# Seven raw weight buffers in place of four, in space taken from the scratch of the software DMAs

## The chip, the cores and the metric

The kernel runs on one core of one Trainium2 chip. The engines of a core work side by side: TensorE (PE in the profile, with its weight loader PEld), VectorE (DVE), ScalarE (ACT), GpSimd (POOL) and SyncE (SP), which here only starts transfers. Sixteen DMA engines move data between HBM and the on-chip memory SBUF. The metric is the device time of one execution in microseconds; lower is better.

## The reference

Two decoder layers over 256 tokens of width 2048, all in float32. The first layer has block attention over 16 heads, the second grouped-query attention (4 shared key/value heads, window 128, a learned sink per head). With 256 tokens and blocks of 256, the first layer's attention is plain causal attention. Each layer ends in a gated feed-forward with a causal depthwise convolution of width 3 between the up projection (2048 to 2 x 5504) and the gate:

```python
h = x
for layer in range(2):
    attn = moba_attention(...) if layer == 0 else swa_attention(...)      # q, k, v, softmax(q k + bias) v, w_o
    h = layer_norm(sqrt(2) * h + attn, ln_g[layer, 0], ln_b[layer, 0])
    ffn = conv_ffn(h, w_up, conv_w, conv_b, w_down)                       # (gelu(conv(h w_up)_g) * conv(h w_up)_v) w_down
    h = layer_norm(sqrt(2) * h + ffn, ln_g[layer, 1], ln_b[layer, 1])
```

Every weight is used once, for 256 tokens: the work is a stream of weights from HBM against a small resident activation.

## The kernel before, in words

**The stream.** The host lays out all weights in the order of use as "halves" of 128 x 1024 float32 (512 KB). There are 704 halves from the input `wst`; 68 more, named `t`, are sums of four blocks of the down projections' weights, which the kernel itself forms in HBM (below). One half after the other goes through three steps:

1. `load_weights` (lines 101 to 109): SP starts the DMA of half `u` into a buffer of the pool `wpool`, which has `RAW_BUFS` = 4 buffers. The tile is `raw`, the DMA is line 106.
2. `high_upto` (line 125): ACT rounds `raw` to the faster matmul format, giving `wh`. `low_piece` (line 134): DVE subtracts, giving the remainder `wl`. These have `HALF_BUFS` = 4 buffers of their own; near the ends of a stage further halves are put into tiles that are free just then (`xT`, `up`, `st`).
3. TensorE multiplies with `wh` and `wl`, three products for each one of float32. In the stages with `ws_unit` (lines 294 and 297), two halves are one unit: 16 matmuls with 512 columns and 16 with 256. The down projections use lines 555 to 557 (`two_chunks`), and their last part, like the value and output projections, lines 347 to 349 (`Moving.mm`).

**Order.** The order of each engine's instructions is written out by the program (`manual_schedule`). `take()` hands out half `i`; before that `split_upto` writes the high and low parts up to half `i + 3`, and after the split of half `s` it writes the next `load_weights`. That next load is half `s + 4` and reuses the buffer of `s`, so it waits on SP until DVE has read it. `at(n, f)` puts other work `n` halves later in this order. SP works through its queue in order, and so a wait there holds what is behind it. Each SP transfer is also given one of eight semaphores in turn, and waits until the transfer that had it before has landed.

**Also on SP:** the pieces of the input `xc` (line 187), tables for the bias, the bias bands of the first layer (lines 278 and 282), the residual input (213), the layer-norm vectors (437).

**The sums.** `plan_sums` spreads over each up projection the making of the sums `t` for the down projection after it (16 for the first layer, 18 for the second, each of two halves). A sum starts with two plain copies on SP (line 261). Then POOL starts three accumulating DMAs in turn (lines 263, 265 and 267), each of which waits for the one before. [...] POOL also starts the second layer's band and bias transfers, four of each in a row, the convolution's weights and some layer-norm vectors; apart from that it does next to nothing.

**Stages in order:** first attention, with its input loaded and split at the start (`load_input`) to 300 us; its output projection to 390; up projection of the first layer to 860; its down projection to 1080; second attention to 1260 and output projection to 1350; second up projection to 1840; second down projection and the final layer norm to the end.

Of the kernel before, what the change touches and what calls it, by code (L numbers as in the profile page):

```python
# [33 lines left out]
SCALE = P ** -0.5  # L34
UL = 384

RAW_BUFS = 4
HALF_BUFS = 4
AHEAD = HALF_BUFS - 1
HW = 1024  # L40
# [34 lines left out]
def trunk(ctx: ExitStack, tc: tile.TileContext, wst, wq, xT_in, x_in, relb, onehot, umask, sinks, conv_in, ln_g, ln_b, out):  # L75
    nc = tc.nc
# [3 lines left out]
    big = ctx.enter_context(tc.tile_pool(name="big", bufs=1))  # L80
    wpool = ctx.enter_context(tc.tile_pool(name="wpool", bufs=RAW_BUFS))
    spool = ctx.enter_context(tc.tile_pool(name="spool", bufs=HALF_BUFS))
# [18 lines left out]
    def load_weights(behind=None):  # L101
        u = todo["load"]
        if u < n_halves:
            raws[u] = wpool.tile([P, HW], F32, name="raw")
            for j, c in enumerate(pieces(u)):
                nc.sync.dma_start(raws[u][:, c], source[u][:, c])
                if behind:
                    behind(j)
            todo["load"] += 1
# [26 lines left out]
    def split_upto(i, behind=None):  # L136
        while todo["low"] <= min(i, n_halves - 1):
            s = todo["low"]
            high_upto(s, behind)
            if len(pieces(s)) == 1:  # L140
                low_piece(s, slice(0, HW))
            placed.pop(s)
            raws.pop(s)
            load_weights()
            todo["low"] += 1
# [4 lines left out]
    def at(n, f, *a, first=False):  # L150

        fs = before.setdefault(slot["now"] + n, [])
        fs.insert(0 if first else len(fs), (f, a))
# [29 lines left out]
    def load_input(pool, tables):  # L183
        xc = pool.tile([P, KB, T], F32, name="xc", bufs=1)

        def load_x(k, n=2, queue=nc.sync):
            queue.dma_start(xc[:, k:k + n], xT_in[:, k:k + n, :])

        def split_x(k, n=2):
            ks = slice(k, k + n)  # L190
            nc.scalar.activation(xT[:, ks, 0:T], xc[:, ks], AF.Copy)  # L191
            nc.vector.tensor_tensor(out=xT[:, ks, T:2 * T], in0=xc[:, ks], in1=xT[:, ks, 0:T].bitcast(F32),
                                    op=ALU.subtract)

        load_weights(lambda j: load_x(j, 1, nc.scalar))
        for u in range(1, RAW_BUFS):
            load_weights()
            if u < 3:
                load_x(u + 1, 1)
        load_x(4)  # L200
        load_x(6)
        tables()
        split_upto(0, lambda j: split_x(j, 1))
        for u in range(1, 3):
            split_upto(u)
            split_x(u + 1, 1)
        for k in range(4, KB, 2):
            if k > 6:
                at(k - 7, load_x, k)
            at(k - 3, split_x, k)  # L210

    def load_residual(t):
        nc.sync.dma_start(res[:, t, :], x_in[t * P:(t + 1) * P, :])
# [518 lines left out]
    def layer_attention(l, rest, stage, turnover):  # L732
# [29 lines left out]
        if l == 0:  # L762
            load_input(pool, lambda: bias_table(pool))
        else:
            nc.vector.tensor_scalar(nsk, sk, -1.0, None, op0=ALU.mult)
# [293 lines left out]
```

## Time and profile before

| | |
|---|---|
| median of 3 runs (lowest, highest) | 2072.65 us (2072.06, 2077.46) |
| the profiled execution, whole | 2069.8 us |
| its span | 2067.6 us |
| busy: TensorE / weight loader / VectorE / ScalarE / GpSimd | 2052.7 / 1771.9 / 1548.5 / 1038.0 / 112.1 us |
| mean granted TensorE clock | 0.998 |
| moved by DMA | 512.07 MB, mean 248 GB/s |
| landing of a raw half from its issue, median | 5.3 us |

In the rows that follow, L12 is line 12 of the kernel, `wh<-raw` is what is written and read, "x" a count, and `A <- B: total, times, longest` says that A sat idle until B. A matmul's end is modelled: consecutive matmuls overlap, so the spacing of their starts tells the pace and the duration does not. SPq is SP's queue. In a row of a stretch, the busy time and count of each engine follow, then the granted clock, the DMA engines' busy share and GB/s. "q1" are transfers of SP, "q0" those of POOL.

### The profile page before, as it was taken

How to read it: one execution, taken by the hardware profiler on the slowest of the kernel's cores; microseconds unless marked ns; L12 is line 12 of the kernel's file. 1: busy time of each engine (PE TensorE's matmuls, PEld its weight loads, DVE VectorE, ACT ScalarE, POOL GpSimd, SP SyncE). 2: the span in 40 equal slices, each digit the busy share in tenths (PEclk: the TensorE clock that was granted, in tenths of full speed). 3: DMA queues.
4: the chain of work that ended last, by engine and by line, in shares of the span. 5: the costliest groups of instructions: out<-in, count | busy, mean ns of one | idle time of the engine just before them, and what ended most of it. 6: DMA issues, size and time to landing. Idle time of an engine off the chain costs nothing.

```text
span 2067.6 us, 29230 instructions
## 1 busy us (share of the span) xinstructions
PE 2052.7 (99%) x10974; PEld 1771.9 (86%) x10974; DVE 1548.5 (75%) x2292; ACT 1038.0 (50%) x1467; POOL 112.1 (5%) x124
## 2 busy tenths in 40 slices
PE   9999999999999999999999999999999999999997
PEld 7888888988888888887888888898888888888886
DVE  5555556788787888877776676788887788886867
ACT  5544444444454455565564555444444445556553
POOL 0000000001111110000000000001111111100000
PEclk9999999999999999999999999999999999999999
DMA  8666548389999998588885544739999999969884
GB/s 320 211 209 210 173 164 280 133 244 288 294 302 274 307 267 263 184 278 294 281 290 195 182 149 160 251 109 302 289 303 309 301 303 262 261 219 308 289 292 160
DMA packets 158445, 512.07 MB, mean 248 GB/s; under 512 B 17840, under 2 KB 22512, under 8 KB 157536
## 3 DMA queue, kind: packets, MB, share of 16 engines
q1 hardware_dynamic: 131168, 456.56, 63.4%
q0 software_dynamic: 26848, 53.39, 15.2%
q8 instruction: 86, 1.41, 0.3%
q14 instruction: 55, 0.45, 0.1%
q10 hardware_dynamic: 288, 0.26, 0.0%
HBM read 507.97 MB, written 86.56 MB: 288 GB/s over the span
## 4 chain that ended last, share of the span: by engine, by line
PE 85%; DMA 8%; DVE 4%; ACT 2%; issue 1%; ACTq 0%; DVEq 0%
PE acc L294 35%; PE acc L297 18%; DMA raw<-in_wst_dram 7%; PE acc L348 5%; PE acc L347 5%; PE acc L349 5%; PE acc L556 3%; PE acc L557 3%; PE acc L555 3%; DVE wl L134 3%; ACT wh L125 2%; PE acc L312 1%; DMA raw<-t 1%; PE at L556 1%; PE at L557 1%; PE at L555 1%
## 5 line engine op out<-in xcount | busy, mean ns | idle before, releaser
L134 DVE TENSOR_TENSOR wl<-raw,wh 128x1024 fp32r<-128x1024 f32 (+1 forms) x716 | 871.2, 1219 | 436.6 <-ACT wh L125 428.0
L125 ACT ACTIVATE wh<-raw 128x1024 fp32r<-128x1024 f32 (+1 forms) x716 | 754.7, 1055 | 681.3 <-DMA raw<-in_wst_dram 309.2
L294 PE MATMUL acc<-xT,wh 128*128 128x512 f32 x3456 | 872.9, 394 | 0.1
L294 PEld LDWEIGHTS acc<-xT,wh 128*128 128x128 f32 x3456 | 623.5, 189 | 113.4 <-ACT wh L125 0.4
L297 PEld LDWEIGHTS acc<-xT,wl 128*128 128x128 f32 x3456 | 471.2, 190 | 34.1 <-DVE wl L134 0.4
L297 PE MATMUL acc<-xT,wl 128*128 128x256 f32 x3456 | 481.8, 282 | 0.0
L556 PE MATMUL acc<-wl,up 128*128 128x512 f32 x336 | 130.9, 390 | 0.8 <-DVE wl L134 0.8
L555 PE MATMUL acc<-wh,up 128*128 128x512 f32 x336 | 130.9, 390 | 0.0
L557 PE MATMUL acc<-wh,up 128*128 128x512 f32 x336 | 130.8, 389 | 0.0
L885 DVE SCALAR_TENSOR_TENSOR work<-work,cw 128x255 f32<-128x255 f32 x172 | 83.2, 484 | 6.1
L886 DVE SCALAR_TENSOR_TENSOR work<-work,cw 128x254 f32<-128x254 f32 x172 | 83.1, 483 | 6.2
L162 ACT ACTIVATE work<-work 128x256 f32<-128x256 f32 x86 | 35.7, 415 | 94.0 <-DVE work L886 93.8
L884 DVE TENSOR_SCALAR work<-work,cw 128x256 f32<-128x256 f32 x172 | 71.6, 417 | 6.2
L556 PEld LDWEIGHTS acc<-wl,up 128*128 128x128 f32 x336 | 63.1, 188 | 14.1 <-DVE wl L134 1.1
L555 PEld LDWEIGHTS acc<-wh,up 128*128 128x128 f32 x336 | 63.1, 188 | 13.6 <-ACT wh L125 0.5
L557 PEld LDWEIGHTS acc<-wh,up 128*128 128x128 f32 x336 | 63.1, 188 | 13.1
L883 DVE TENSOR_TENSOR work<-acc,work 128x256 f32<-128x256 f32 x172 | 71.7, 417 | 1.5 <-ACT work L882 1.5
L882 ACT ACTIVATE work<-acc 128x256 f32<-128x256 f32 x172 | 62.6, 364 | 6.5 <-PE acc L324 6.5
L347 PE MATMUL acc<-wh,xT 128*128 128x512 f32 x144 | 57.6, 400 | 0.6 <-ACT xT L191 0.6
L263 POOL DMA_DIRECT2D t<-in_wq_dram x34 | 44.4, 1305 | 240.4 <-DMA t<-in_wq_dram 240.3
L265 POOL DMA_DIRECT2D t<-t x34 | 35.1, 1032 | 397.6 <-DMA t<-in_wq_dram 361.9
L348 PE MATMUL acc<-wl,xT 128*128 128x512 f32 x144 | 56.3, 391 | 0.0
(208 smaller groups left out, 2148.0 us busy)
## 6 DMA issues: line engine op xcount, KB each, us to landing
raw<-in_wst_dram SPq DMA_DIRECT2D x704, 512.0 KB, 5.3
t<-in_wq_dram SPq DMA_DIRECT2D x68, 512.0 KB, 8.9
raw<-t SPq DMA_DIRECT2D x68, 512.0 KB, 4.7
t<-in_wq_dram POOLq DMA_DIRECT2D x34, 512.0 KB, 12.7
t<-t POOLq DMA_DIRECT2D x34, 512.0 KB, 9.4
t<-in_wq_dram POOLq DMA_DIRECT2D x34, 256.0 KB, 7.7
gb<-in_ln_g_dram POOLq DMA_DIRECT2D x2, 1024.0 KB, 10.5
gb<-in_ln_b_dram POOLq DMA_DIRECT2D x2, 1024.0 KB, 13.4
```

The source lines that it names most:

```text
L125: nc.scalar.activation(wh[:, c], raws[s][:, c], AF.Copy)
L134: nc.vector.tensor_tensor(out=wl[:, c], in0=raws[s][:, c], in1=wh[:, c].bitcast(F32), op=ALU.subtract)
L294: nc.tensor.matmul(acc, cols(wh, j), xT[:, k, :], start=(k == 0), stop=False)
L297: nc.tensor.matmul(o, cols(wl, j), xT[:, k, 0:T], start=False, stop=(k == KB - 1))
L347: nc.tensor.matmul(acc, sh, wh, start=(k == 0), stop=False)
L348: nc.tensor.matmul(acc, sh, wl, start=False, stop=False)
L349: nc.tensor.matmul(acc, sl, wh, start=False, stop=(k == self.nk - 1))
L555: nc.tensor.matmul(bank(key), a[0], wh[:, c], start=key not in begun, stop=False)
L556: nc.tensor.matmul(bank(key), a[0], wl[:, c], start=False, stop=False)
L557: nc.tensor.matmul(bank(key), a[1], wh[:, c], start=False, stop=stop)
L885: nc.vector.scalar_tensor_tensor(c[:, 1:T], h[:, 0:T - 1], w[:, 1:2], c[:, 1:T], op0=ALU.mult, op1=ALU.add)
L886: nc.vector.scalar_tensor_tensor(c[:, 2:T], h[:, 0:T - 2], w[:, 0:1], c[:, 2:T], op0=ALU.mult, op1=ALU.add)
```

## The change

The raw pool gets seven buffers of 4 KB a partition in place of four. The 12 KB for that come from the DMA scratch, which is set to 4 KB. At the start four halves are loaded ahead as before; three further `load_weights` calls are put in the order after halves 16, 19 and 22. From there on the load written after the split of half `s` is half `s + 7`. Since buffers rotate by seven from the first half on, the fifth to seventh loads find free buffers and have no split to wait for. Every tile allocated before the raw pool lies 12 KB lower; those after it stay.

```diff
-RAW_BUFS = 4
+RAW_FIRST = 4
+RAW_BUFS = 7
+DMA_SCRATCH = 4096
...
         load_weights(lambda j: load_x(j, 1, nc.scalar))
-        for u in range(1, RAW_BUFS):
+        for u in range(1, RAW_FIRST):
             load_weights()
...
             at(k - 3, split_x, k)
+        for i in range(RAW_BUFS - RAW_FIRST):
+            at(16 + 3 * i, load_weights)
...
-    nc = _bacc.Bacc("TRN2", target_bir_lowering=False, num_devices=1)
+    nc = _bacc.Bacc("TRN2", target_bir_lowering=False, num_devices=1, dynamic_dma_scratch_size=DMA_SCRATCH)
```

## The prediction

> **What bounds the kernel now.** I read the page first, then who waited for whom (all engines, then the weight loader and SP's queue), the matmul counts by stretch, and the order of time around the few places where TensorE waits. The page:
>
> ```profile
> span 2067.6 us, 29230 instructions
> PE 2052.7 (99%) x10974; PEld 1771.9 (86%) x10974; DVE 1548.5 (75%) x2292; ACT 1038.0 (50%) x1467; POOL 112.1 (5%) x124
> ...
> DMA  8666548389999998588885544739999999969884
> ...
> raw<-in_wst_dram SPq DMA_DIRECT2D x704, 512.0 KB, 5.3
> ```
>
> TensorE (PE) looks busy for 99% of the span, but its ends are modelled, so I check that with matmul counts. The two long stretches in which the DMA engines are fullest are the up projections; line 294 is 16 of a unit's 32 matmuls:
>
> ```profile
> 416.00:860.00 444.00, 318.71 (x1272) 228.69 (x1272) 1.00 0.93 273
> 1390.00:1830.00 440.00, 315.70 (x1262) 226.55 (x1260) 1.00 0.98 287
> ```
>
> 444 us over 1272/16 units is 5.585 us a unit; 440 over 1262/16 is 5.578. The second stretch has a higher DMA share (0.98 against 0.93) and is no slower. The matmuls set this pace, and a fuller queue has not moved it. The granted clock is 1.00 in both.
>
> Now what the weight buffers cost. Columns: us in total, times, longest.
>
> ```profile
> ACT wh L125 <- DMA raw<-in_wst_dram: 309.2, 245, 5.0
> ...
> ACT wh L125 <- DMA raw<-t: 37.2, 44, 2.7
> ...
> PE acc L556 <- DVE wl L134: 0.8, 1, 0.8
> ...
> PE acc L348 <- DVE wl L134: 0.4, 1, 0.4
> ```
>
> ScalarE (ACT) waits 309.2 + 37.2 = 346 us for raw weights; TensorE waits 1.2 us. Between them stand the four `wh`/`wl` pairs, three halves ahead, which is some 8 us of matmul. So the raw ring is late all the time for ACT and hardly ever for the engine that sets the end. The weight loader shows the same waits before the matmul queue smooths them:
>
> ```profile
> PEld acc L556 <- DVE wl L134: 1.7, 3, 1.1
> ...
> PEld acc L348 <- DVE wl L134: 1.1, 2, 0.8
> PEld at L556 <- DVE wl L134: 0.9, 3, 0.4
> ...
> PEld acc L555 <- ACT wh L125: 0.5, 1, 0.5
> PEld acc L294 <- ACT wh L125: 0.4, 2, 0.3
> PEld acc L297 <- DVE wl L134: 0.4, 2, 0.2
> ```
>
> The two large ones, in order of time (start, duration):
>
> ```profile
> 949.68 0.39 PE L557 MATMUL acc<-wh,up 128*128 128x512 f32 x1
> ...
> 950.11 0.49 PE L555 MATMUL acc<-wh,up 128*128 128x512 f32 x1
> ...
> 951.37 0.50 PE L556 MATMUL acc<-wl,up 128*128 128x512 f32 x1 [0.76 <-DVE wl L134]
> ...
> 951.71 0.40 PE L557 MATMUL acc<-wh,up 128*128 128x512 f32 x1
> ...
> 951.95 0.40 PE L555 MATMUL acc<-wh,up 128*128 128x512 f32 x1
> ```
> ```profile
> 2042.81 0.39 PE L347 MATMUL acc<-wh,up 128*128 128x512 f32 x1
> ...
> 2043.61 0.50 PE L348 MATMUL acc<-wl,up 128*128 128x512 f32 x1 [0.41 <-DVE wl L134]
> ...
> 2043.94 0.40 PE L349 MATMUL acc<-wh,up 128*128 128x512 f32 x1
> ```
>
> Matmuls of this shape otherwise start 0.23 us apart (951.71 to 951.95 is 0.24). From 949.68 to 951.71, three steps that should take 0.69 took 2.03: 1.34 lost. From 2042.81 to 2043.94, two steps took 1.13 in place of 0.46: 0.67 lost. Together 2.0 us.
>
> **The change, part by part.**
>
> *The ring of seven.* Nothing is computed more or less. All engines but SP keep the order of their instructions; SP issues the same loads, earlier. Why ACT waits now is in the chain of waits, one turn of the ring:
>
> ```profile
> 897.74 5.54 DMA raw<-in_wst_dram
> ...
> 903.39 1.07 ACT wh L125
> ...
> 904.48 1.24 DVE wl L134
> ...
> 905.73 5.02 DMA raw<-in_wst_dram
> ```
>
> Load, high half, low half, then the freed buffer's next load: 905.73 − 897.74 = 7.99 us for four halves, 2.00 us a half. With seven buffers the same turn gives 1.14 us a half, and one transfer alone has the next bound: 512 KB at the 296 GB/s of the fullest stretch is 1.77 us. So in the down projections a half can come about 0.2 us sooner, until the ring is full, and each stage is entered with three more halves in hand (three times about 2.3 us). ACT's wait for raw should mostly go; late next are its waits for a free `wh` buffer, that is for TensorE. What TensorE gets back: the 2.0 us above, and part of the small waits. The loader rows that wait on `wh` or `wl`, without the 0.3 us of line 348 that lies in the opening, sum to 1.7 + 0.8 + 0.9 + 0.5 + 0.4 + 0.4 = 4.7; of that, 2.4 (0.5 + 1.1 + 0.8) belongs to the two places counted. The other 2.3 lies in small waits, which a loader one matmul ahead partly absorbs; I take half, 1.2. Gain: 2.0 + 1.2 = **3.2 us**, between 2.0 and 4.7.
>
> *Three more loads, after halves 16, 19 and 22.* Three DMA issues of about 0.33 us on SP, which does nothing else. 3 × 512 KB is 4.9 us of DMA at the opening's rate, and in the order written the loads 4 to 6 no longer wait for a split, so they go out at once behind the first four:
>
> ```profile
> 0.00:50.00 50.00, 48.02 (x210) 39.15 (x211) 27.83 (x34) 26.81 (x35) 2.95 (x10) 1.00 0.89 321
> 9.11 8.12 SPq L106 DMA_DIRECT2D raw<-in_wst_dram  x5
> ```
>
> They ride SP's queue, behind everything needed sooner, and SP reaches the input pieces queued after them no later than now. Cost 0; if their transfers did push the input back, up to 4.9 us.
>
> *Order past SP's queue.* SP also carries the first two transfers of each sum (line 261), the bias table, the residual and the layer-norm vectors. They keep their place in the order but land behind up to three more halves, some 5 us (3 × 1.77). The sums have long cover, below; the others are loaded stages ahead.
>
> *SP's own limits.*
>
> ```profile
> SPq L106 <- DVE wl L134: 695.7, 373, 8.9
> ...
> SPq L106 <- DMA raw<-in_wst_dram: 81.2, 65, 3.5
> ```
>
> SP waits mostly for a split to free a buffer. But 65 times it waited for an earlier load to land: the written order gives each SP transfer one of eight semaphores, which the transfer eight places before must have released. During the sums two of nine SP transfers are not weights, so about six of the seven buffers can be in flight there. In the down projections nearly all seven.
>
> *The scratch cut to 4 KB* concerns POOL's DMAs alone. They hardly overlap: each of a sum's three waits for the one before. If less room made POOL wait at the four band spreads that it issues in a row, nothing on TensorE's path follows; POOL is 5% busy. Cost 0; it is dear only where the sums come late, the second rival.
>
> *Tiles move by 12 KB* in SBUF. No row shows a cost of place:
>
> ```profile
> L125 ACT ACTIVATE up<-raw x30: 1043/1061/1064, 329.5 to 1349.8; 128x1024 fp32r<-128x1024 f32 x30
> L134 DVE TENSOR_TENSOR up<-raw,up x30: 1207/1225/1228, 330.6 to 1365.2; 128x1024 fp32r<-128x1024 f32 x30
> ```
>
> Over all the places it rotates through, the split spreads by 21 ns. On engines at 50% and 75% that is 0 us; either way it is below what can be measured.
>
> *Sum.* The profiled execution took 2069.8 us, its span 2067.6 and 2.2 around it; minus 3.2 is 2066.6. The median of the three runs, 2072.65, stands 2.85 above it, so in the terms of the median: **2069.4 us**. A difference under 0.3%, 6.2 us, is about what a measurement of this kernel cannot tell from none.
>
> **Rivals.**
>
> *The ring does not help (2072.65).* If the late halves are late for bandwidth, more buffers only queue earlier. For: a DMA share of 0.9 to 1.0 over half the span. Against: ACT waits for raw in the down projections with the chain turning at 2.00 us a half against 1.77 that the engines could do.
>
> *SP's longer queue starves the sums (slower).* POOL builds each quad's sum by three accumulating DMAs, each waiting for the last; they share the DMA engines with SP.
>
> ```profile
> L267 POOL DMA_DIRECT2D t<-in_wq_dram x18: 817/827/842, 1418.6 to 1809.5; - x18
> DMA to landing us min/median/max: 6.2/7.9/9.4
> L106 SPq DMA_DIRECT2D raw<-t x36: 326/326/327, 1827.2 to 2006.2; - x36
> ```
> ```profile
> 560.00:640.00 80.00, 80.00 (x462) 70.45 (x461) 63.87 (x103) 37.67 (x56) 9.52 (x10) 1.00 1.00 296
> q1 hardware_dynamic: 5234, 19.07, 63.9%
> q0 software_dynamic: 2391, 4.54, 35.9%
> ```
>
> A sum of the second layer takes (1809.5 − 1418.6)/17 = 23.0 us now. The last is read at 2006.2, so it may take (2006.2 − 9.4 − 1418.6)/17 = 34.0 before a load, with SP's whole queue behind it, waits. At 36 it is 17 × 2 = 34 us late: 2069.4 + 34 = 2103. For it: the engines are full (share 1.00) and SP's queue grows from four to seven loads; if the engines served by what is outstanding, POOL's transfers would slow by up to 7/4, to 40 us a sum. Against: the other queue already has work nearly all the time and POOL's still gets 35.9%.
> [...]
>
> *The unprofiled excess is weights too (faster).* If the 2.85 us by which the median exceeds the profiled run is more of these stalls, and all 4.7 go: 2072.65 − 2.85 − 4.7 = 2065.1. Nothing profiled shows it.
>
> *The opening pays 4.9 us* while the gain stays: 2069.4 + 4.9 = 2074.3.
>
> **How the numbers follow.** Forecast 0.55; no help 0.22; starved sums 0.09; excess too 0.09; opening 0.04; some cost of place or scratch with no row, 0.01. Within 0.3% (2066.4 to 2078.9): 0.55 + 0.22 + 0.04 = 0.81; faster 0.09; slower 0.10. The range goes from the excess case, 2065, to the opening's with no gain, 2072.65 + 4.9 = 2078; starved sums stay out.
>
> **What would show it.** Right: ACT's wait for raw falls from 346 us to below 120, its wait for TensorE's matmuls rises; the holes at 950 and 2043 are gone; units stay at 5.58 us; raw loads take longer to land (5.3 now) without harm. Wrong: a unit above 5.6 us in the up projections; POOL's last sum after 2000; SP waiting at `raw<-t` for POOL's transfers; holes in the first 50 us that now show none after the start.

## The result, and the profile after

The changed kernel takes 2065.53 us (median of 7 runs, 2065.39 to 2065.95). The kernel before, run beside it, takes 2072.94 us (7 runs, 2071.2 to 2080.96). The ratio is 0.9958, with a 95% interval of 0.9944 to 0.9972: 7.4 us or 0.42% faster. The forecast was 2069.4 us and "within 0.3%". The gain has the right sign and is more than twice the forecast's 3.2 us. The time lies at the low end of the range that the prediction gave, and 0.42% is past the 0.3% to which it gave most of its chances. The seven runs of the kernel before are few for a kernel whose runs spread by 10 us: in the later comparisons, with 11 to 26 runs each, its median lies between 2071.25 and 2072.59 us, so the gain is some 6 to 7 us.

The profiled execution took 2065.53 us. Its lines are numbered anew: the load is line 108 (it was 106), ACT's rounding 127 (125), DVE's 136 (134), the units 298 and 301 (294 and 297), the value and output projections 351 to 353 (347 to 349), the down projections 559 to 561 (555 to 557). Its page:

```profile
span 2063.3 us, 29227 instructions
...
PE 2050.3 (99%) x10974; PEld 1772.7 (86%) x10974; DVE 1543.7 (75%) x2292; ACT 1052.5 (51%) x1467; POOL 112.7 (5%) x124
...
DMA  9666558389999998688884545639999999989883
...
PE 99%; DVE 0%; POOL 0%; issue 0%; ACT 0%; POOLq 0%
...
raw<-in_wst_dram SPq DMA_DIRECT2D x704, 512.0 KB, 5.4
```

The last row but one is the chain that ended last, by engine: followed back from the end, it now stays on TensorE for 99% of the span. In the profile before, the same row was

```profile
PE 85%; DMA 8%; DVE 4%; ACT 2%; issue 1%; ACTq 0%; DVEq 0%
```

so 14% of that span lay off TensorE, nearly all of it on raw loads (8%) and the two steps of the split (5%). Little of this is lost time: the table below finds 4.27 us. The same two stretches of the up projections, and who holds ScalarE now (total, times, longest):

```profile
416.00:860.00 444.00, 318.36 (x1273) 228.66 (x1272) 1.00 0.93 273
1390.00:1830.00 440.00, 314.93 (x1258) 225.90 (x1257) 1.00 0.98 287
```
```profile
ACT wh L127 <- PE acc L298: 245.2, 224, 2.4
...
ACT wh L127 <- PE acc L561: 130.6, 149, 1.7
...
ACT wh L127 <- DMA raw<-in_wst_dram: 17.4, 15, 3.2
```

The units are where they were (444 us over 1273/16 is 5.58). ScalarE's wait for raw weights fell from 346 to 17.4 us; what it waits for is TensorE. The two holes, at 949.7 and 2042.8 before, are gone; the matmuls there start 0.23 us apart:

```profile
948.29 0.39 PE L561 MATMUL acc<-wh,up 128*128 128x512 f32 x1
948.51 0.39 PE L559 MATMUL acc<-wh,up 128*128 128x512 f32 x1
948.74 0.39 PE L560 MATMUL acc<-wl,up 128*128 128x512 f32 x1
...
2039.25 0.39 PE L351 MATMUL acc<-wh,up 128*128 128x512 f32 x1
2039.47 0.39 PE L352 MATMUL acc<-wl,up 128*128 128x512 f32 x1
```

**Where TensorE got time back.** Both kernels run the same 10,974 matmuls in the same order. So the start of the k-th matmul in one trace minus its start in the changed kernel's shows, stage by stage, what was lost. The table has us lost against the changed kernel's profile; "rings of 5 to 7" are the three experiments below with only ring and scratch changed, and the ring of seven without its calls.

| stage (us in the changed kernel) | before | before, a second profile | rings of 5 to 7 |
|---|---|---|---|
| opening and first attention (0 to 300) | 0.41 | 2.56 | −0.17 to 0.56 |
| output projection, layer norm (to 390) | 0.00 | 0.00 | 0.00 |
| first up projection (to 860) | 0.63 | 0.00 | 0.00 |
| first down projection (to 1080) | 2.53 | 3.19 | 0.00 |
| second attention, second up projection (to 1840) | 0.00 | 0.00 | 0.00 |
| second down projection and end | 0.71 | 5.14 | 0.00 |
| sum | 4.27 | 10.89 | −0.17 to 0.56 |

Of the 4.27 us of the profile before, 2.0 are the two holes, 1.86 are small waits, and 0.41 lie in the opening, where the rings differ among themselves by as much.

**Why four buffers are just too few in the down projections.** A stretch of the first down projection in the changed kernel, the halves that ScalarE rounds in it, and the same stretch before:

```profile
900.00:1030.00 130.00, 130.00 (x575) 107.65 (x574) 96.30 (x88) 75.83 (x73) 0.00 (x0) 1.00 0.88 302
```
```profile
L127 ACT ACTIVATE wh<-raw x71: 1046/1062/1067, 900.0 to 1029.0; 128x1024 fp32r<-128x1024 f32 x71
```
```profile
900.00:1030.00 130.00, 129.20 (x565) 105.29 (x564) 94.25 (x91) 73.54 (x71) 0.00 (x0) 1.00 0.88 292
```

With nothing in its way TensorE does 575 matmuls in 130 us, 0.226 us each, and uses up 71 halves: one every 1.83 us. One turn of a ring of four is a landing, 1.07 us of ScalarE and 1.24 of VectorE (the prediction's rows) and about 0.1 of gaps. In the trace before, the median landing of a half from `wst` is 4.5 us from 950 to 1085 us (its row stands at the sums, below), 4.7 over the whole stage (870 to 1080) and 5.0 in the stretch shown. At 4.5 the turn is 6.9 us, or 1.73 a half: 5% faster than TensorE. At 4.7 it is 1.78, and at 5.0 it is 1.85: slower than TensorE. With five buffers, landings of 4.5 and 5.0 give 1.38 and 1.48. In the up projections a half is needed every 5.58/2 = 2.79 us, and four buffers lose next to nothing there. The turns are worked out from medians; how uneven landings add up to the loss of one execution was not followed wait by wait.

### The profile page after: what moved, and what is told of

It is laid out like the page before. It is cut to its first block, busy times and chain, and to the rows that moved or that the text cites. A ratio compares the mean times of both kernels' runs of the same rounds, so it can differ in the third digit from the quotient of the medians.

```text
span 2063.3 us, 29227 instructions
## 1 busy us (share of the span) xinstructions
PE 2050.3 (99%) x10974; PEld 1772.7 (86%) x10974; DVE 1543.7 (75%) x2292; ACT 1052.5 (51%) x1467; POOL 112.7 (5%) x124
## 4 chain that ended last, share of the span: by engine, by line
PE 99%; DVE 0%; POOL 0%; issue 0%; ACT 0%; POOLq 0%
PE acc L298 39%; PE acc L301 20%; PE acc L351 5%; PE acc L353 5%; PE acc L352 5%; PE acc L559 5%; PE acc L560 5%; PE acc L561 5%; PE at L559 1%; PE at L560 1%; PE at L561 1%; PE acc L316 1%; PE acc L328 1%; PE at L686 1%; PE at L719 1%; PE at L712 1%
## 5 line engine op out<-in xcount | busy, mean ns | idle before, releaser
L351 PE MATMUL acc<-wh,xT 128*128 128x512 f32 x144 | 57.9, 402 | 0.0
L269 POOL DMA_DIRECT2D t<-t x34 | 35.4, 1040 | 391.1 <-DMA t<-in_wq_dram 341.8
L353 PE MATMUL acc<-wh,xT 128*128 128x512 f32 x144 | 56.2, 390 | 0.0
```

The costliest lines, as they stand in the source:

```text
L351: nc.tensor.matmul(acc, sh, wh, start=(k == 0), stop=False)
L353: nc.tensor.matmul(acc, sl, wh, start=False, stop=(k == self.nk - 1))
```

## Experiments

The theory is that TensorE loses time where the four-buffer ring brings raw weights late, that this varies from execution to execution, and that any ring with a little slack removes all of it. Rivals: the three extra calls or the depth of seven do it; the sums' traffic does it; the cut scratch or the shifted places cost or gain something. Each result has the median [lowest to highest] and the ratio to the kernel before, run beside it, with its 95% interval. Where a diff has no comment it stands against the changed kernel; "..." marks what is left out.

### Depth: five, six and seven buffers, with and without the calls

```diff
-RAW_BUFS = 7
+RAW_BUFS = 5
```

> The changed kernel with five buffers. A turn of the ring of about 8.0 us gives 1.60 us a half in place of 2.00. Theory A1 (the four-buffer turn is just too slow for the down projections): 1.60 is already below the 1.77 us that the transfer itself takes at 296 GB/s, so five buffers give most of the gain: 2065.5 to 2067.5 us, a ratio of 0.9965 to 0.9975. Theory A2 (the depth of the cushion against uneven landings counts): about a third of the gain, near 2070.5 us, a ratio of 0.9988.

Measured: 2065.69 us [2065.5 to 2066.26], 0.9973 [0.9963, 0.9984]. Five buffers do all that seven do. The rows that show it, chain by engine and ScalarE's wait for raw:

```profile
PE 99%; DVE 0%; DMA 0%; ACT 0%; issue 0%
```
```profile
ACT wh L127 <- DMA raw<-in_wst_dram: 38.6, 34, 4.1
```

ScalarE still waits twice as long for weights as with seven, and TensorE sees none of it.

```diff
-        for i in range(RAW_BUFS - RAW_FIRST):
-            at(16 + 3 * i, load_weights)
```

> Seven buffers without the three extra calls after halves 16, 19 and 22, so that the order of SP's queue stays as before and only the buffer that each load waits for is another. Theory A (SP runs through its order as soon as the buffer is free): the full gain, 2065.5 us, a ratio of 0.996, and loads that are issued some 17 us ahead of their split in the up projections. Theory C (the three calls make the lead): no gain, 2072.9 us, a ratio of 1.000, and a lead of some 8 us as before.

Measured: 2065.72 us [2065.41 to 2066.07], 0.9973 [0.9962, 0.9984]. Without the three calls nothing is lost: SP runs ahead in its queue until a buffer is not free (its waits for `wl`, the end of a split, sum to 687.0 us here and to 677.7 in the changed kernel), so the ring fills by itself.

```diff
-RAW_BUFS = 7
-DMA_SCRATCH = 4096
+RAW_BUFS = 5
+DMA_SCRATCH = 12288
```

> Five buffers and 12 KB of scratch: the least that buys one buffer. Theory A (one more buffer is what counts): 2065.5 us as with seven, spread under 1 us. Rival (with five, it was the small scratch that helped, by spacing POOL's transfers): back toward 2071 us.

Measured: 2066.0 us [2065.37 to 2066.81], 0.9975 [0.9967, 0.9984].

```diff
-RAW_BUFS = 7
-DMA_SCRATCH = 4096
+RAW_BUFS = 6
+DMA_SCRATCH = 8192
```

> Six buffers and 8 KB of scratch. Theory A: 2065.5 us, the same as five and seven, since TensorE has nothing left to wait for. For POOL's band spreads: if a spread needs more than half of 4 KB, 8 KB lets two or three go out at once, and POOL waits at one or two of the four in place of three.

Measured: 2065.79 us [2065.35 to 2066.17], 0.9975 [0.9966, 0.9984]. Five, six and seven cannot be told apart. One more buffer, 4 KB a partition, is the whole of the gain.

### The kernel before, profiled again

> The kernel before, unchanged, for a second profile. Theory A (the runs of before differ by how long TensorE waits for late raw weights): its span is above 2067.6 us if this execution is a longer one, and the difference to the changed kernel's matmul starts grows at waits for wh or wl, in the same stages as in the first profile (up projection of the first layer, down projections), while the stretches between them stay equal to 0.1 us. Rival D (the runs differ by something outside the matmul stream: launch, start, clock): the difference to the changed kernel's starts stays 4.3 us and the rest lies outside the span or is spread evenly.

Measured: 2071.54 us [2068.68 to 2076.78], 1.0007 [0.9997, 1.0017]. This execution took 2076.43 us, with a span of 2074.2 against 2067.6 in the first profile. The table above splits it: 10.89 us lost instead of 4.27. The difference, 6.62, is the difference of the two spans. 5.1 us of it lie in the down projections, 2.15 in the opening and the first attention, and the first up projection lost 0.63 us less. The loader's waits of the second profile:

```profile
PEld at L556 <- DVE wl L134: 3.8, 9, 0.7
PEld acc L556 <- DVE wl L134: 3.7, 6, 1.1
PEld acc L348 <- DVE wl L134: 2.5, 3, 1.1
```

These three lines were 0.9, 1.7 and 1.1 in the first. So the first profile showed the kernel before in one of its better executions. Over all runs it took 2067.1 to 2081.0 us, while no kernel with five or more buffers left 2065.3 to 2066.9.

The loss in the opening is late weights too. It lies at two places. At 36.8 us TensorE waits for `wh` and then `wl` of a half that landed late (1.27 us lost). At 52.6 it waits for `vt` (1.20 lost), which ACT writes only after a `wh` whose raw half took 9.1 us to land. From the chain of the second profile (start, duration):

```profile
41.79 9.11 DMA raw<-in_wst_dram
...
51.00 1.06 ACT wh L125
52.06 0.49 ACT vt L796
...
52.60 2.14 PE acc L294 x8
```

A third profile of four buffers, the last kernel below (default scratch, four transfers of the second layer left out), lost 8.88 us in a run of 2073.88 us, 8.42 of it in the down projections. So what sets the median of the kernel before above its first profile is more of the same waits.

### One buffer fewer: three

Against the kernel before.

```diff
-RAW_BUFS = 4
+RAW_BUFS = 3
```

> The kernel before with three buffers. Theory V: a turn takes landing plus 2.4 us of splits plus issue. In the down projections, with landings near 4 us, 6.5/3 = 2.2 us a half against the 2.0 to 2.7 that TensorE needs, in the up projections, with landings of 6 us or more beside the sums, 8.5/3 = 2.8 against 2.79: losses in both, 20 to 60 us in all, 2092 to 2130 us. Rival A2 (only uneven single landings matter, not the pace of the turn): a few more single waits, 2075 to 2085 us, and the up projections still at 5.58 us a unit.

Measured: 2284.76 us [2280.1 to 2291.0], 1.1035 [1.1019, 1.1051]. The direction is right; the loss of 213 us is over three times the top of the expected 20 to 60. The chain in the first up projection (start, duration) shows a part of the turn that the expectation left out:

```profile
594.22 9.32 DMA raw<-in_wst_dram
...
603.64 1.06 ACT wh L125
...
604.73 1.23 DVE wl L134
605.95 0.34 DVE work L883
...
607.81 0.06 DVE work L889
...
609.40 6.14 DMA raw<-in_wst_dram
```

Between the split and the next load VectorE also does the convolution (`work`), and the landings are 6 to 9 us. Two turns take 609.40 − 594.22 = 15.2 us and then 12.0 to the next load at 621.41: 4 to 5 us a half, where 2.79 is wanted. These turns are among the long ones: from 520 to 880 us the mean is 3.24 us a half (890 matmuls of line 294, 16 for two halves). The convolution is not all that was left out. Of the 225.5 us that the profile lost against the changed kernel, 55 lie in the first up projection, 70 in the second attention, its output projection and the second up projection, and 83 in the down projections, in which the convolution does next to nothing. There the expectation's own 2.2 us a half stands against a need of 1.83, not of 2.0 to 2.7. A further part is the clock: TensorE's mean granted clock was 0.985 over the span of 2288.8 us, in the changed kernel 0.998 over 2063.3. If it was either 1.00 or 0.50, as in the rows of the last section, that is an estimated 69 us at 0.50 against 8, and the 60 us more can account for up to half of that, 30 us. The depth has a knee: 213 us between three and four buffers, about 6 between four and five, nothing beyond.

### The sums' traffic

The kernel before, without the planned sums; the down projections read blocks of `wq` as they are where they would read sums. The sums and their traffic are left out.

```diff
-    tsum = {q: dram.tile([2, P, HW], F32, name=f"t{i}") for i, q in enumerate(QUAD_LIST)}
+    def block_of(l, n, p, i):
+        return wq[QUAD_LIST.index((l, n, p))][:, i:i + 2, :].rearrange("p a b -> p (a b)")
...
-            source += [tsum[l, n, h[1]][h[2]] if h[0] == "t" else wst[next(used)] for h in quad_halves(l, n)]
+            source += [block_of(l, n, h[1], h[2]) if h[0] == "t" else wst[next(used)] for h in quad_halves(l, n)]
...
-            plan_sums(l, 12, (4 * FT - 30) // (sum(QUADS[l]) + 3))
```

> The kernel before, four buffers and 16 KB, without making the sums: the halves t are read straight from blocks of the input wq, so the output is not the reference's, but every load, split and matmul of the stream stays, and some 120 GB/s of other traffic leaves the up projections. Theory U (the sums' traffic makes the raw weights late): all waits go, 2065.5 us, spread under 1 us. Theory V (the turn of four buffers is too slow in the down projections, where no sums are made): the waits of the up projection (0.6 us) go, those of the down projections stay, 2069 to 2072 us, with runs several us apart.

Measured: 2083.01 us [2080.87 to 2087.31], 1.0061 [1.0048, 1.0074]: slower, which neither theory had. The up projections lost 0.00 us, so the sums' traffic had cost at most the 0.63 us seen there in the first profile. The loss is in the down projections, 7.97 and 6.96 us. The landings from 950 to 1085 us (KB, median us), with the sums first and without second:

```profile
raw<-in_wst_dram SPq DMA_DIRECT2D x57, 512.0 KB, 4.5
raw<-t SPq DMA_DIRECT2D x15, 512.0 KB, 4.5
```
```profile
raw<-in_wst_dram SPq DMA_DIRECT2D x55, 512.0 KB, 5.0
raw<-in_wq_dram SPq DMA_DIRECT2D x15, 512.0 KB, 5.0
```

In this stretch half a microsecond more per landing carries the turn from 1.73 to 1.85 us a half, across TensorE's 1.83. Over the whole stage (870 to 1080) it is 0.3 us more, 5.0 against 4.7, which carries the turn from 1.78 to 1.85. The run takes 11.5 us longer. The reason for the longer landings was not isolated; the blocks of `wq` are read in another pattern than the sums. The same with five buffers and 12 KB of scratch:

> The kernel without the sums (halves t read straight from blocks of wq, so the output is not the reference's), with five buffers and 12 KB of scratch. Theory V (the turn of the ring alone): 2065.5 us, spread about 1 us, a fall of 17 us for one buffer, with the landings in the down projections as long as with four. Rival (reading wq itself is what slows the down projections): the loss stays for a large part, above 2072 us.

Measured: 2065.94 us [2065.73 to 2066.84], 0.9971 [0.9962, 0.9979]. The landings are as long, 4.9 and 5.4 us, and the 17 us are gone. This is the plainest sign that what counts is the ring's slack, not the traffic itself.

### The scratch and the places

Four buffers with the scratch of 4 KB. In the first kernel every tile lies 12 KB lower than in the kernel before; in the second an unused tile of 12 KB holds the places of the kernel before:

```diff
-RAW_BUFS = 7
+RAW_BUFS = 4
```

> The changed kernel with the ring set back to four; the scratch stays at 4 KB, and everything lies 12 KB lower. Theory A (the ring covers late raw weights): as before, about 2072.9 us, a ratio of 1.000, and single runs that again lie up to 8 us apart. Theory B (the smaller scratch or the new places give the gain): about 2065.5 us, a ratio of 0.996. Both: POOL's four band spreads go out one at a time, as in the changed kernel, if the small scratch is what spaces them.

```diff
-RAW_BUFS = 7
+RAW_BUFS = 4
...
+    pad = ctx.enter_context(tc.tile_pool(name="pad", bufs=1)).tile([P, 3072], F32, name="pad")
+    nc.vector.memset(pad[:, 0:1], 0.0)
```

> Four buffers and 4 KB of scratch, with the freed 12 KB left empty below the tiles, so that every tile lies where it lay before. Theory P (the places cost what the four-buffer, 4 KB kernel loses): the loss goes, a ratio of 1.000 to the kernel before. Theory Q (the small scratch costs it, by band spreads that go out one at a time until about 366 us and slow the raw loads behind which the first output projection's normalization stands): the loss stays, a ratio of 1.003, the band spreads are 11 to 13 us apart, and TensorE waits some 2 to 3 us for the normalization near 384 us.

Measured: 2077.88 us [2073.29 to 2080.66], 1.003 [1.0021, 1.0039], and 2075.85 [2073.73 to 2080.31], 1.0024 [1.0012, 1.0035]. The two intervals overlap: no cost of the places can be told. Both are slower than before by 0.24 to 0.3%, where both theories of the first kernel had 1.000 or less: in a ring of four the small scratch has a price. It lies in one place, a wait of TensorE for the first layer's layer norm (2.67 us lost from 300 to 390 in the first, 6.66 in the second, 0.00 before). Ahead of it POOL starts the four band spreads of the second layer. POOL's queue in the second kernel, then before (start, duration):

```profile
314.05 1.11 POOL L284 DMA_DIRECT2D band<-ud  x1
325.34 1.09 POOL L284 DMA_DIRECT2D band<-ud  x1 [10.18 <-issue]
339.64 1.07 POOL L284 DMA_DIRECT2D band<-ud  x1 [13.21 <-issue]
352.05 1.08 POOL L284 DMA_DIRECT2D band<-ud  x1 [11.35 <-issue]
```
```profile
314.43 4.32 POOL L278 DMA_DIRECT2D band<-ud  x4
```

With 4 KB they start 11.3 to 14.3 us apart, about the 12.6 us (median) that one takes to land, in place of 1.1, so they last to about 365 us in place of 330. In that time (314 to 366 us) the raw loads land in 7.0 us (median) instead of 4.6, and 22 are issued instead of 25. With seven buffers they take 8.2 and 28 are issued: it is harmless there.

To see whether the spreads are the cause, I first wrote them later in the order. The diff stands against the second kernel above.

```diff
-            if self.l == 0:
-                for h in range(0, NH, 4):
-                    spread_bias(1, h, h + 4)
...
+            if l == 0:
+                for i in range(4):
+                    at(1 + 2 * i, spread_bias, 1, 4 * i, 4 * i + 4)
```

> The kernel with four buffers, 4 KB of scratch and the old places, with one edit: the four band spreads of the second layer go out during the opening of the first up projection, where the DMA engines are a third busy, in place of the first output projection. Theory Q (the spaced spreads in the output projection are the price of the small scratch): the wait of 4 to 7 us between 300 and 390 us goes, and the ratio comes back to 1.000, about 2071.3 us. Rival (the small scratch costs by the sums or in the down projections): the ratio stays 1.0024, about 2076 us, with no wait between 300 and 390.

Measured: 2078.92 us [2075.42 to 2085.01], 1.0041 [1.0027, 1.0055]. This tested nothing: POOL waits for no one there and started them at 315 us, much as before, so it is a repeat of the second kernel (6.98 us lost from 300 to 390). Next the same spreads on SP, whose queue does hold them back (the last starts at 422.2 us); this diff stands against the kernel just shown:

```diff
-        (nc.gpsimd if l else nc.sync).dma_start(band[l, h0:h1], bass.AP(tensor=a.tensor, offset=a.offset + P - 1,
+        nc.sync.dma_start(band[l, h0:h1], bass.AP(tensor=a.tensor, offset=a.offset + P - 1,
```

> Four buffers, 4 KB of scratch, the old places; the four band spreads of the second layer now go through SP's queue, between the loads of the first up projection's opening, so that they use no scratch and come after the output projection (in the attempt before, POOL ran ahead and sent them out at 314 us as ever). Theory Q (the spaced spreads in the output projection are the price of the small scratch): no wait between 300 and 390 us, and a ratio near 1.000, about 2071.5 us. Rival (the small scratch costs elsewhere): no wait there, but a ratio of 1.002 to 1.004.

Measured: 2080.48 us [2076.32 to 2085.06], 1.0034 [1.0022, 1.0046]. By its time the rival had it, but the trace shows where the time goes: the loss from 300 to 390 is 0.00, and a new one of 8.1 us stands from 415 to 500, where the spreads now are. The wait moved with them. Another 4.9 us are lost at three waits for `wh` from 700 to 760, whose cause no run settles. So this kernel does not decide between the two. Last, without the four spreads, the second layer reading the first layer's band (so its bias is another): with the 4 KB scratch and the held places, and with the default scratch in the kernel before.

```diff
-        (nc.gpsimd if l else nc.sync).dma_start(bias[:, h0:h1, :], band[l, h0:h1].rearrange("h q j -> q h j"))
+        (nc.gpsimd if l else nc.sync).dma_start(bias[:, h0:h1, :], band[0, h0:h1].rearrange("h q j -> q h j"))
...
-            if self.l == 0:
-                for h in range(0, NH, 4):
-                    spread_bias(1, h, h + 4)
```

> Four buffers, 4 KB of scratch, the old places, and the four band spreads of the second layer left out altogether (the second layer reads the first layer's bias, so the output is not the reference's). Theory Q (the spaced spreads are the whole price of the small scratch): no wait between 300 and 390 us or in the opening after it, and the same time as the next kernel with 16 KB, a ratio of 0.999 to 1.000. Rival (the small scratch costs elsewhere, in the sums): a ratio of 1.002 or more, and above the next kernel's.

> The kernel before, 16 KB of scratch, with the same four spreads left out (output again not the reference's). The spreads cost nothing before, so both theories give the ratio 1.000, about 2071.5 us; it is the measure for the kernel with 4 KB.

Measured: 2073.03 us [2069.73 to 2075.84], 1.0002 [0.9993, 1.0011], and 2072.23 [2069.91 to 2075.49], 1.0002 [0.9993, 1.001]. Both lose 0.00 us from 300 to 860. Without the spreads the small scratch costs nothing that can be told. They are its whole price, and of the rings of four, five and seven that were run with 4 KB only that of four pays it.

## Why the prediction was wrong

**What bounds the kernel: right.** TensorE sets the pace, late raw weights were what it lost, and a deeper ring covers them. Units, holes and ScalarE's waits came out as foretold. That raw loads would take longer to land did not: 5.4 us against 5.3.

**"In the terms of the median": this step failed.** It took the 2.85 us by which the median stood above the profiled execution for a constant, and so subtracted a gain read from one execution. The distance was more of the same waits, and it is gone: the changed kernel's median and its profiled execution are both 2065.53 us. The measured 7.41 us are the forecast's 3.2, then 1.07 by which the profiled pair gained more than that (4.27), the 2.85, and 0.29 by which the median of seven runs of the kernel before stands above that of three. This is the rival "the unprofiled excess is weights too", which gave 2065.1 us and had 0.09; the median is 2065.53. Its form holds (the excess goes), its sum less exactly: it added all 4.7 of the loader's waits outside the opening, and the profiled pair lost 3.87 there and 0.41 in the opening. Nor was a difference under 0.3% beyond telling: the interval of the ratio is 0.28% wide, and the runs of the changed kernel spread by 0.03%.

**What would have told it from the rows on hand.** The prediction compared the ring's turn of four (7.99 us, 2.00 a half) with its estimate of 1.77 for a transfer at 296 GB/s (the opening of the changed kernel moves 349), and never with what TensorE wants in the down projections, for which it had only a rough 2.3 us. The stretch from 900 to 1030 gives 1.83 (in the trace before, with its small losses, 69 halves in the same 130 us, or 1.88). A ring that supplies one in 1.73 to 2.00 us against a need of 1.83 has no slack, and then the loss can depend on how the landings of one execution fall. The three runs shown, up to 2077.46, already hinted at such a spread.

**The small waits: too low.** Half of 2.3 us was taken as reaching TensorE; 1.86 did. The two holes were right at 2.0.

**Three more loads, order past SP, SP's limits: right, cost 0.** The calls are not needed at all. But six or seven loads in flight at a time did not come: with landings of 4.7 us and a half every 1.83, fewer than three are under way in the down projections (4.7/1.83 = 2.6), and the other buffers hold halves that have landed. SP's 65 waits on an earlier landing became four:

```profile
SPq L108 <- DMA raw<-in_wst_dram: 2.6, 4, 0.9
```

**The scratch: right for this kernel, wrong in its reason.** That POOL might wait at the band spreads was foreseen; "nothing on TensorE's path follows" is false with four buffers (0.24 to 0.41% in three kernels) and holds only since the ring is deeper. How a slower landing there leads to a late layer norm was read from the landings and the waits; that the spreads cause it was shown. That the scratch holds back POOL's transfers and not SP's is seen in the changed kernel, with its 4 KB: from 314 to 366 us POOL's four spreads start 11.4 to 13.7 us apart and land in 12.5 (median), while SP issues 28 loads that land in 8.2, an estimated four at a time (28 × 8.2/52 = 4.4).

**The places: right.** The first two kernels with four buffers and the small scratch differ by less than their intervals.

**Starved sums: did not come.** The last of the three accumulating DMAs of the second layer's sums, and POOL's share from 560 to 640 us:

```profile
L271 POOL DMA_DIRECT2D t<-in_wq_dram x18: 820/829/839, 1417.6 to 1821.5; - x18
```
```profile
q0 software_dynamic: 2343, 4.46, 35.4%
```

A sum takes (1821.5 − 1417.6)/17 = 23.8 us instead of 23.0, far from 34.0, and POOL's share is 35.4% against 35.9. But the rival's premise did not come either: SP's queue grew no longer. In that stretch a raw half lands in 7.6 us (median) before and after, and 28 were issued before, 29 after, because a buffer comes free at TensorE's pace whatever the depth of the ring. So how the engines share between a long and a short queue was not tested. The packets in that stretch were 5234 of SP to 2391 of POOL before, and 5247 to 2343 after.

**The opening:** it paid nothing that can be told from its own variation of −0.17 to 0.56 us.

## What to carry to other kernels

Divide one turn of a ring (landing, processing, freeing) by its buffers and compare that with the consumer's time per buffer, stage by stage. Here the two came within a few per cent of each other in the down projections; the ring was the source of the loss and of the run-to-run spread, and one buffer more removed both. When the runs of a kernel spread by more than its changes are worth, do not read a gain from one profiled execution: ask which waits could make the spread, and profile it again. When scratch or buffers are traded, look for the one stage in which the smaller resource was in use, and ask what covers it after the trade.

## What was not expected of the hardware

One wait of TensorE cost nearly twice its length. In the kernel with four buffers, the small scratch and held places, TensorE waited once for the layer norm, for 3.8 us, and lost 6.66 there. By stretch (PE, weight loader, DVE, ACT, POOL, then granted clock, DMA share, GB/s):

```profile
382.00:384.00 2.00, 0.00 (x0) 0.00 (x0) 1.57 (x5) 0.29 (x1) 0.00 (x0) 0.91 0.90 270
384.00:386.00 2.00, 1.24 (x5) 1.25 (x6) 1.97 (x3) 0.03 (x1) 0.00 (x0) 0.50 0.27 111
386.00:388.00 2.00, 2.00 (x6) 1.52 (x6) 1.97 (x4) 0.57 (x1) 0.00 (x0) 0.50 0.00 0
388.00:390.00 2.00, 2.00 (x9) 1.60 (x8) 1.61 (x3) 0.60 (x1) 0.00 (x0) 0.50 0.00 0
...
392.00:394.00 2.00, 2.00 (x12) 1.66 (x11) 0.69 (x1) 1.78 (x3) 0.00 (x0) 1.00 0.00 0
```
```profile
384.76 1.12 PE L602 MATMUL at<-ident,res 128*128 128x128 f32 x4 [3.79 <-DVE res L593]
...
386.95 0.63 PE L353 MATMUL acc<-up,st 128*128 128x512 f32 x1
387.38 0.63 PE L354 MATMUL acc<-up,st 128*128 128x512 f32 x1
```

The granted clock fell to 0.50 for 6.8 us, in which matmuls start 0.43 us apart in place of 0.23. In the kernel with the spreads on SP the longest wait was 6.3 us, and the clock was 0.88 from 435 to 440 us, in which TensorE was busy for 0.86, and 0.50 from 440 to 445. In the one with the spreads later in the order it was 4.5 us, with 6.98 lost; its mean clock is 0.997, as in the kernel above, and 0.998 in the kernel before. In the kernel with every tile 12 KB lower, the wait was 2.45 us, and the clock stayed at 1.00 (2.67 lost).

Among these four the clock fell with the longer waits. The ring of three does not fit an order by length: one of its stretches at 0.50 follows 3.41 us in which TensorE was idle for 1.95 in all (3.41 − 1.46). In the columns of the rows above:

```profile
717.42:720.83 3.41, 1.46 (x6) 1.22 (x7) 1.23 (x1) 2.01 (x3) 1.03 (x1) 1.00 0.49 184
720.83:724.25 3.42, 3.42 (x13) 3.06 (x13) 2.87 (x5) 1.65 (x3) 0.00 (x0) 0.50 0.82 137
```

So 1.95 us of idle time stand before a stretch at 0.50 there, and 2.45 before none in the kernel with every tile 12 KB lower. What decides it was not shown.

The second thing is the scratch. The four transfers of the second layer's band, 512 KB each, were issued 11 to 14 us apart with 4 KB, where one took some 12.5 us to land (median). With 8 KB three went out within 3.3 us and the fourth after 8.4 us of waiting; with 12 and 16 KB all four went out within 4.3 us. POOL did not fail, it waited.
